# SwiGLU on one core: the first tile loaded with 32 KiB descriptors, all other full tiles with 64 KiB

## The chip, the cores and the metric

The kernel runs on one core of a Trainium2 chip. The time is the device time of one execution in microseconds (us). A kernel's executions are timed in rounds beside executions of the kernel before on the same chip. With one core there is no second die to compare.

## The reference

The input is one float32 matrix of 8192 x 8192 (268.44 MB), the output one of 8192 x 4096 (134.22 MB).

```python
a, b = np.split(x, 2, axis=-1)
silu_b = b / (1 + np.exp(-b))
return a * silu_b
```

## The kernel before

Two rows of the input share one partition, so a tile is 128 partitions x 16,384 floats, or 64 KiB per partition and 8 MiB in all. There are 32 tiles and three buffers. Loads are issued from the sync engine (SP), stores of tiles 0 to 29 from GpSimd, and the last stores again from SP. ScalarE computes SiLU in place, VectorE multiplies in place, and the store reads from the same buffer. A buffer is loaded again when its store has landed.

```python
    def load(i, rows=None):
        if i not in tiles:
            tiles[i] = pool.tile([P, R * M], x.dtype, name="xt")
        lo, hi = (0, R) if rows is None else rows
        nc.sync.dma_start(
            out=tiles[i][:, lo * M : hi * M], in_=xv[i * P : (i + 1) * P, lo * M : hi * M]
        )
    # ... swiglu(i, k): activation (SiLU), then tensor_mul; store(i): dma_start
    for i in range(BUFS):
        load(i)
    for i in range(last):
        for k in range(R):
            swiglu(i, k)
        if i == last - 1:
            swiglu(last, 0)
        store(i)
        nxt = i + BUFS
        if nxt < last:
            load(nxt)
        elif nxt == last:
            load(last, (0, 1))
            load(last, (1, 2))
    # ... the last tile is computed and stored in pieces
```

## Time and profile before

| | before |
|---|---|
| median of the three first runs | 936.34 us |
| span of the profiled run | 934.3 us |
| VectorE, ScalarE, GpSimd busy | 30%, 25%, 2% |
| bytes moved, mean rate over the span | 402.68 MB, 431 GB/s |
| SP's data queue (q1), GpSimd's data queue (q0) | 68.6% and 31.2% of 16 engines' span |

"Share of 16 engines' span" is the time that a queue's packets took, divided by sixteen times the span. Two shares that add up to nearly 100% say that the transfer engines are full, and then it matters little who waits for whom. A packet in the trace is here one descriptor, that is one contiguous run in one partition, and I use the two words for the same thing.

### The profile page before, as it was taken

The page shows a single profiled execution, that of the slowest core. Times are in us where ns is not written, and L with a number is a line of the kernel's source. Part 1 is how long each engine was busy: PE and PEld are TensorE (multiplying, and loading weights), DVE is VectorE, ACT ScalarE, POOL GpSimd, SP SyncE. Part 2 cuts the span into 40 slices and gives each one's busy share as a digit, 9 for nine tenths or more (in the row PEclk, how much of TensorE's full clock was granted, in tenths as well). Part 3 has the DMA queues.
Part 4 walks back from the last instruction along what each step waited for, and adds up shares of the span by engine and source line. Part 5 has one row for each costly group of instructions (what it writes and reads, how often), then busy time and mean ns, then how long its engine had stood idle before and what let it go on. Part 6 is the DMA issues. An engine that isn't in the chain of part 4 may idle for free.

```text
span 934.3 us, 400 instructions
## 1 busy us (share of the span) xinstructions
DVE 283.3 (30%) x65; ACT 229.4 (25%) x66; POOL 16.3 (2%) x34
## 2 busy tenths in 40 slices
DVE  0333312333113332133321333213333133331252
ACT  0323330233311333113331133311333203332041
POOL 0000000000000000000000000000000000000000
DMA  9999999999999999999999999999999999999998
GB/s 404 404 449 426 425 448 424 436 429 446 428 422 441 432 446 424 446 415 453 428 421 456 415 452 421 427 450 415 442 428 441 429 435 428 438 450 414 437 432 383
DMA packets 9507, 402.68 MB, mean 431 GB/s; under 512 B 1056, under 2 KB 1056, under 8 KB 1056
## 3 DMA queue, kind: packets, MB, share of 16 engines
q1 hardware_dynamic: 5184, 276.83, 68.6%
q0 software_dynamic: 4320, 125.83, 31.2%
q14 instruction: 3, 0.02, 0.0%
HBM read 268.44 MB, written 134.22 MB: 431 GB/s over the span
## 4 chain that ended last, share of the span: by engine, by line
DMA 84%; DVE 10%; ACT 4%; issue 1%; DVEq 0%; SPq 0%; ACTq 0%
DMA out_dram<-xt 43%; DMA xt<-in_x_dram 40%; DVE xt L51 10%; ACT xt L50 4%; DVEq L106 0%; SPq L43 0%; ACTq L50 0%; DVEq L51 0%
## 5 line engine op out<-in xcount | busy, mean ns | idle before, releaser
L51 DVE TENSOR_TENSOR xt<-xt 128x4096 f32<-128x4096 f32 (+1 forms) x65 | 283.3, 4359 | 636.9 <-ACT xt L50 633.7
L50 ACT ACTIVATE xt<-xt 128x4096 f32<-128x4096 f32 (+1 forms) x65 | 228.1, 3556 | 687.3 <-DMA xt<-in_x_dram 687.3
L58 POOL DMA_DIRECT2D out_dram<-xt x30 | 16.1, 537 | 854.8 <-DVE xt L51 854.8
L50 ACT ACT_TABLE_LOAD x1 | 1.3, 1283 | 0.7 <-PEq L95 0.7
L95 POOL MEMSET const-float32-0.0<- 128x1 f32 x1 | 0.1, 99 | 0.2 <-issue 0.2
L95 POOL MEMSET const-bfloat16-1.0<- 128x1 bf16 x1 | 0.1, 102 | 0.0
L95 POOL MEMSET const-float32-1.0<- 128x1 f32 x1 | 0.1, 99 | 0.0
L95 POOL MEMSET const-uint8-127<- 128x1 uint8 x1 | 0.1, 99 | 0.0
## 6 DMA issues: line engine op xcount, KB each, us to landing
out_dram<-xt POOLq DMA_DIRECT2D x30, 4096.0 KB, 40.5
xt<-in_x_dram SPq DMA_DIRECT2D x2, 4096.0 KB, 26.4
out_dram<-xt SPq DMA_DIRECT2D x1, 4096.0 KB, 23.8
out_dram<-xt SPq DMA_DIRECT2D x2, 2048.0 KB, 14.5
xt<-in_x_dram SPq DMA_DIRECT2D x31, 33.5
```

What stands on the lines that cost most here:

```text
L50: nc.scalar.activation(out=b, in_=b, func=_SILU)
L51: nc.vector.tensor_mul(out=xt[:, k * half + c0 : k * half + c0 + cw], in0=xt[:, k * M + c0 : k * M + c0 + cw], in1=b,)
L58: (nc.gpsimd if i < last - 1 else nc.sync).dma_start(out=ov[i * P : (i + 1) * P, c0 : c0 + cw], in_=tiles[i][:, c0 : c0 + cw])
L95: nc = _bacc.Bacc("TRN2", target_bir_lowering=False, num_devices=1)
```

## The change

The intent can be read from the diff: only the first tile is cut into smaller descriptors, at the one place where the pipeline has nothing else to do. The loads of the other tiles keep their 64 KiB per partition in one piece.

```diff
         lo, hi = (0, R) if rows is None else rows
+        desc = 4 * M if i == 0 else 4 * R * M
         nc.sync.dma_start(
-            out=tiles[i][:, lo * M : hi * M], in_=xv[i * P : (i + 1) * P, lo * M : hi * M]
+            out=tiles[i][:, lo * M : hi * M],
+            in_=xv[i * P : (i + 1) * P, lo * M : hi * M],
+            max_dma_last_dim=desc,
         )
```

## The prediction

> **What bounds the kernel now.** I began with the header of the page and its parts 1 to 3, to see whether an engine or the transfers set the time.
>
> ```profile
> span 934.3 us, 400 instructions
> DVE 283.3 (30%) x65; ACT 229.4 (25%) x66; POOL 16.3 (2%) x34
> DMA  9999999999999999999999999999999999999998
> DMA packets 9507, 402.68 MB, mean 431 GB/s; under 512 B 1056, under 2 KB 1056, under 8 KB 1056
> q1 hardware_dynamic: 5184, 276.83, 68.6%
> q0 software_dynamic: 4320, 125.83, 31.2%
> ```
>
> The busiest compute engine works 30% of the span, while the 16 DMA engines are at 90% or more in every slice but the last. The two data queues together fill 68.6% + 31.2% = 99.8% of the engines' time. The kernel must read 268.44 MB and write 134.22 MB whatever it does, so the bytes bound it, not a wait. The packet records give the rate of one engine: a 64 KiB packet takes 2,418 ns, a 32 KiB packet 1,213 ns (the same for loads and stores), a 16 KiB packet 611 ns. I counted 3,968, 4,224 (3,840 of them GpSimd's stores) and 256 of these. The sum is 9,594.6 + 5,123.7 + 156.4 = 14,874.7 us, or 929.7 us on each of 16 engines. That is within 5 us of the span of 934.3.
>
> Next I read the chain that ended last, at its start, because the change touches only the first tile.
>
> ```profile
> 0.74 0.38 SPq L43
> 1.13 0.06 issue
> 1.18 43.55 DMA xt<-in_x_dram
> 44.75 3.62 ACT xt L50
> 48.40 4.43 DVE xt L51
> 52.93 4.44 DVE xt L51
> 57.66 41.39 DMA out_dram<-xt
> ```
>
> The first 43.55 us of the chain are not the load of tile 0 but that of tile 1, which waits behind tile 0 in the same queue. ScalarE first starts at 22.72 us, when tile 0 has landed, and the chain doesn't pass through that point. The chain's shares by line (43% stores, 40% loads) name waits for data that moves at the full rate; they don't mean that a shorter latency would pay.
>
> Last, the places where engines move less than full rate, since only those can still be won or lost. Columns: window, its length, DVE, ACT and POOL busy with counts, clock, DMA share, GB/s. Packets are counted lumpily in short windows, so I read only the direction.
>
> ```profile
> 2.00:5.00 3.00, 0.00 (x0) 0.02 (x1) 0.00 (x0) 1.00 0.75 306
> 38.00:43.00 5.00, 0.00 (x0) 0.00 (x0) 0.00 (x0) 1.00 0.98 308
> 100.00:900.00 800.00, 247.81 (x56) 199.43 (x56) 14.39 (x27) 1.00 1.00 434
> ```
>
> Steady state is 434 GB/s for 800 us. There are two dips. At the start, first packets begin between 1.75 and 2.62 us and take 3.06 us in the mean instead of 2.42: 0.64 us of extra latency per engine. Around 38.6 to 43 us, one load packet on each engine takes 3.77 us in the mean instead of 2.42, just before the very first store packet (42.16 us): 1.36 us per engine, once. It is the last packet of tile 1. Later stores show no such dip, presumably because their queue no longer runs empty. Elsewhere I assigned packets to engines by end and start, and found two gaps above 150 ns in the whole run, neither above 310 ns. So all that is left beyond pure movement is about 1.8 us before the first byte, 0.64, 1.36, and some 1.5 us after the last byte (932.8 to 934.3).
>
> **What the Trainium skill says.** "DMA: Bandwidth & Descriptors", section "Where 436 GB/s comes from", gives a fabric ceiling of 435 GB/s for the 16 ports. The 434 above agrees, so this kernel has no rate left to find. The same page, section "Why a DMA increments its semaphore by 16 and not by 1", says that one descriptor moves one contiguous run of the last dimension, and that the number of engines follows from the slowest dimension. The changed load has the form 128x2x8192 in place of 128x16384, so 128 still leads and all 16 engines should be used; it becomes 256 descriptors, 16 per engine instead of 8. The trace of before agrees in so far as 31 full loads left 31 x 128 = 3,968 packets of 64 KiB. Third, section "Queues, rings and completion order" says that each engine alternates between queues by packet, so packet size can set the shares of two queues. No run yet shows that for tile 0, and it has no rival queue: its last completion is at 20.6 us after the first packet, about 22.4 us into the span, and the first store packet comes at 42.16. Fourth, "Perfetto Trace Analysis", section "DMA Instruction — HWDGE (DVE, Sync)", says that the issue seen in the profile is the generation of descriptors. In this trace one issue of 128 descriptors takes 0.33 us (0.38 for the first).
>
> **The change part by part.** The listing of instructions shows the same count and order on every engine; the only difference is the shape of the first load. All other loads have 64 KiB per partition in one piece before and after (the last tile's two halves have 32 KiB anyway), so naming the limit changes nothing there.
>
> Removed: 128 packets of 64 KiB, 8 per engine. Added: 256 packets of 32 KiB, 16 per engine. Two small packets cost 2 x 1,213 = 2,426 ns against 2,418, so 8 ns more per pair. The 611 ns of the 16 KiB packet confirms a fixed 8 to 9 ns per packet (2 x 611 - 1,213 = 9). On each engine that is 8 x 8 = 64 ns. The DMA engines are the bound and never idle, so these 0.06 us go straight to the end.
>
> The second term is the generation of descriptors. If the issue scales with their number, the first one grows from 0.38 to about 0.7 us (an estimate, from the issue durations above). The issues of tiles 1 and 2 come later by 0.3 us, hidden behind 19 us of queued work. Whether the first packet waits for all descriptors of the load is not shown; first packets appear at 1.75 us on most engines, but at 2.62 us on the last. If the engines are fed in turn, twice the descriptors could move the late ones by up to 0.4 us, and lateness persists, since every engine has the same bytes to move. I charge 0.1 us, between none and 0.4.
>
> Nothing is subtracted. Compute waits for the semaphore of the whole tile, not for half of a row, so a smaller descriptor makes nothing available earlier. Sum: +0.06 + 0.1 = about +0.2 us, giving 936.34 + 0.2 = 936.5.
>
> **The rivals.** *A faster start.* The intent may be that the pipeline fills sooner when the first packet is half as long. For it: the first packets are the slow ones. Against it: their excess, 0.19 to 1.02 us by engine, looks like a latency before the first byte, and not like a packet that must be read whole before it is written; for that, the excess would have to be close to 2.4 us. If half the excess did scale with size, the gain would be 0.3 us: 936.0. *A different first store.* The 1.36 us dip could depend on how the queue stands when the first store arrives. For it: it is the largest loss in the run. Against it: tile 0's descriptors are gone 20 us before, and tiles 1 and 2 keep theirs. A different phase could make it 0.5 us shorter or longer: 935.8 to 937.0. *Half the bytes in flight at the start.* If 32 KiB reads kept the memory less busy, tile 0 would load below full rate. The last tile's 32 KiB loads ran at 1,213 ns per packet, that is full rate, so I give this little; at a loss of 2% in tile 0's 19.4 us it would be +0.4 us: 936.7.
>
> **Range and chances.** The three runs of before lie within 0.65 us, so noise is about 0.35 us either way. The rivals move the time by -0.5 to +0.7 us. Together an 8 in 10 range of 935.6 to 937.4. A change of 2% is 18.7 us, about the whole transfer of tile 0; with the bytes unchanged at the ceiling rate I see no way to win that, and a loss would need a fault such as fewer engines. Chances: faster 1%, within 2% 98%, slower 1%.
>
> **What would show it.** In the changed profile: 128 packets of 64 KiB gone and 256 of 32 KiB there, so q1 has 5,312 packets for the same 276.83 MB; tile 0's 32 KiB packets at 1,213 ns after the first; ScalarE's first start within 0.3 us of 22.72; the first issue near 0.7 us (or 0.38, if the issue does not scale); the dip before the first store again about 1.4 us; the last packet ending within 1 us of 932.8. I would be wrong if tile 0 used fewer engines or ran below full rate, if its packets took more than 1,300 ns, or if the engines' order after the start changed such that new gaps of over 0.3 us appeared later on.

## The result, and the profile after

The changed kernel took 935.98 us (median of 6 runs, 935.78 to 936.51). The kernel before took 935.93 us (6 runs, 935.80 to 936.64). The ratio is 1.000, with a 95% interval of 0.9987 to 1.0013. A ratio is the mean time of one kernel's runs over that of the other's of the same rounds, so it is not quite the ratio of the medians. A difference of 0.05 us cannot be told from none.

Lines from the page of the changed kernel (header and parts 2 and 3):

```profile
span 934.7 us, 400 instructions
DMA  9999999999999999999999999999999999999998
DMA packets 9635, 402.68 MB, mean 431 GB/s; under 512 B 1056, under 2 KB 1056, under 8 KB 1056
q1 hardware_dynamic: 5312, 276.83, 68.6%
q0 software_dynamic: 4320, 125.83, 31.2%
```

SP's queue has 5,312 packets instead of 5,184, which are the 128 extra ones, for the same 276.83 MB and the same share. The row of transfer engines is as full as before.

The start of the chain that ended last, of the changed kernel (start, duration, what; some short steps left out):

```profile
0.74 0.44 SPq L44
1.18 0.06 issue
1.24 43.29 DMA xt<-in_x_dram
44.55 3.62 ACT xt L53
48.20 4.43 DVE xt L54
52.73 4.44 DVE xt L54
57.46 41.40 DMA out_dram<-xt
```

Step by step this is the chain of before. The first issue takes 0.44 us instead of 0.38. Tile 1 is ready at 44.55 instead of 44.75 us, and tile 0 (not on this chain) at 22.81 instead of 22.72.

The same three stretches as in the prediction, for the changed kernel (window, length, VectorE, ScalarE and GpSimd busy with counts, clock, DMA share, GB/s):

```profile
2.00:5.00 3.00, 0.00 (x0) 0.02 (x1) 0.00 (x0) 1.00 0.73 273
38.00:43.00 5.00, 0.00 (x0) 0.00 (x0) 0.00 (x0) 1.00 0.96 315
100.00:900.00 800.00, 247.55 (x56) 199.43 (x56) 14.34 (x27) 1.00 1.00 434
```

The 800 us in the middle run at 434 GB/s in both kernels. The two dips at the start stand where they stood. The lower 273 beside 306 in the first window says nothing of the change: a second trace of the kernel before gives 218 there. By the packet records, tile 0 landed 0.08 us later than before (22.44 against 22.36 us).

The packet records of the trace, in two pairs (the second pair was taken later, as r_before and r_after; see the experiments):

| | before | before again | after | after again |
|---|---|---|---|---|
| tile 0's packet, steady duration | 2,418 ns | 2,418 ns | 1,213 ns | 1,213 ns |
| first packets, over the steady duration | 0.64 us | 0.78 us | 0.77 us | 0.59 us |
| tile 0 landed (last engine) | 22.36 us | 22.61 us | 22.44 us | 22.31 us |
| dip at the first store, per engine | 1.36 us | 1.17 us | 1.17 us | 1.19 us |
| last data packet ended | 932.76 us | 933.10 us | 933.22 us | 932.70 us |

"First packets, over the steady duration" is the mean over the 16 engines. "Dip" is the excess of each engine's one stretched load packet over 2,418 ns, averaged over the engines.

Two traces of one and the same kernel differ by up to 0.25 us in the rows of the start and by 0.34 and 0.52 us in the last row, which is more than the change can make. Had I had only the first pair, I could have told a story in which a shorter dip pays for slower first packets. The second pair takes it away.

### The profile page after: what moved, and what is told of

It is laid out like the page before. It is cut to its first block, busy times and chain, and to the rows that moved or that the text cites. A ratio compares the mean times of both kernels' runs of the same rounds, so it can differ in the third digit from the quotient of the medians.

```text
span 934.7 us, 400 instructions
## 1 busy us (share of the span) xinstructions
DVE 283.3 (30%) x65; ACT 229.4 (25%) x66; POOL 16.3 (2%) x34
## 3 DMA queue, kind: packets, MB, share of 16 engines
q1 hardware_dynamic: 5312, 276.83, 68.6%
## 4 chain that ended last, share of the span: by engine, by line
DMA 84%; DVE 10%; ACT 4%; issue 1%; DVEq 0%; SPq 0%; ACTq 0%
DMA out_dram<-xt 43%; DMA xt<-in_x_dram 41%; DVE xt L54 10%; ACT xt L53 4%; DVEq L109 0%; SPq L44 0%; ACTq L53 0%; DVEq L54 0%
```

## The experiments

The theory is that the 16 transfer engines are full from the second to the 933rd microsecond, so a change of descriptors costs or wins the fixed time per packet, times the packets per engine, and nothing else. The rivals are that the start of the pipeline has slack or can be shortened, that packet sizes set the shares of the two queues and so the waits, and that the dip at the first store moves with the change. Each kernel below gave correct results.

### All full tiles in 32 KiB pieces (e1_all_32k)

```diff
-        desc = 4 * M if i == 0 else 4 * R * M
+        desc = 4 * M
```

> All full loads in 32 KiB pieces (31 tiles rather than the first alone). Theory (the engines are full, so each extra packet costs its fixed 8 ns, and nothing else counts): 31 x 8 x 8 ns = 2.0 us more than before, 937.9 against 935.9, with no gaps above 150 ns beyond a handful. Rival (packet size sets the shares of the two queues, and that shapes the waits): loads fall from two bytes in three to one in two while a store is queued, stores land sooner than 40 us after issue, and the time moves by something other than 2 us, more than 4 us either way. Rival (size is free): 935.9, unchanged.

It took 937.55 us (6 runs, 937.42 to 941.53) against 935.94 (11 runs); the ratio of the means is 1.0027 (1.0015 to 1.0040), pulled up by two long runs out of six (939.66 and 941.53). By the medians this is 1.6 us more for 31 tiles, by the means 2.6 us, against 2.0 expected. So one tile's share is 0.05 to 0.08 us. The shares of the queues did change, as the rival had it: SP's waits for a buffer, which were 28.5 to 28.6 us nearly throughout before, now alternate between about 21 and 36 us. But the time did not move by the 4 us or more that this rival needed. The profile fell on the run of 939.66 us, and it shows some twenty-five single packets stretched by 0.25 to 0.84 us between 564 and 915 us, so that the engines ended unevenly (their last completions lie 2.4 us apart, against 1.2 before). Eighteen of them lie where GpSimd's queue starts again after 17 us without a packet (at 564.49, 622.71, 680.79, 738.82, 797.10 and 855.64 us). At the eight earlier starts of this kind, from 99.18 to 506.65 us, no packet was stretched by more than 0.01 us. Why the later ones and not the earlier I do not know.

### All loads in 8 KiB pieces (e2_all_8k)

```diff
-        desc = 4 * M if i == 0 else 4 * R * M
+        desc = 8192
```

> All loads, the last halves too, in 8 KiB pieces. Theory: 28,544 more load packets, at 8 to 9 ns each over 16 engines, 14 to 16 us more: 950 to 952 us, ratio 1.015 to 1.017; an 8 KiB packet takes about 310 ns (9 + 2,409/8). Rival (queue shares): stores now take four bytes in five while both queues have work, the stores land in half the time, loads bunch up, and the time is off that sum by more than 5 us.

It took 951.25 us (4 runs, 951.18 to 951.49) against 935.94, ratio 1.0164 (1.0149 to 1.0178). That is 15.3 us more, in the middle of the expected 14 to 16. An 8 KiB packet took 312 ns. The cost per extra packet is 15.3 x 16 / 28,544 = 8.6 ns, the same 8 to 9 ns as from the packet durations of the first trace. Lines from the page of this kernel (parts 2, 3 and 6; the last is stores: count, KB each, median us from issue to landing):

```profile
DMA  9999999999999999999999999999999999999998
DMA packets 38051, 402.68 MB, mean 424 GB/s; under 512 B 1056, under 2 KB 1056, under 8 KB 1056
q1 hardware_dynamic: 33728, 276.83, 69.7%
q0 software_dynamic: 4320, 125.83, 30.7%
out_dram<-xt POOLq DMA_DIRECT2D x30, 4096.0 KB, 16.6
```

The rival of the queue shares was half right: the stores land in 16.6 us, where the kernel before shows

```profile
out_dram<-xt POOLq DMA_DIRECT2D x30, 4096.0 KB, 40.5
```

and yet the time stays on the packet sum, and not 5 us off it.

The reader should see that a slower kernel looks just as full in the busy row: "9" means that packets were in work, not that they were as large as they could be. Only the GB/s and the packet count tell the two apart. (The rounded shares of its two queues add up to 100.4%, since packets of one engine overlap by some nanoseconds in the records.)

### The first tile alone in 1 KiB and in 8 KiB pieces (e3_first_1k, e3b_first_8k)

```diff
-        desc = 4 * M if i == 0 else 4 * R * M
+        desc = 1024 if i == 0 else 4 * R * M      # e3b: 8192
```

> The change exaggerated: the first tile alone in 1 KiB pieces, 64 per partition, 512 per engine instead of 8. Theory: a cost in tile 0 goes straight to the end although the chain that ended last does not pass through tile 0's landing: 504 extra packets x 8 to 9 ns = 4.0 to 4.5 us, so 940 to 940.5 us, ScalarE's first start 4 us later than 22.7. Rival (tile 0's landing has slack, because the chain starts with tile 1's load): no more than 0.5 us, 936.4. Rival (generation of descriptors is what a smaller piece costs): the first issue grew by 0.06 us for 128 more descriptors; at that price 8,064 more cost 3.8 us in the issue, and if the engines wait for it, the first packets come late.

> The first tile alone in 8 KiB pieces, a middle dose, for the trace only. Theory: 56 extra packets per engine x 8 to 9 ns = 0.5 us, too small for a time but readable in the landing of tile 0 (22.9 us instead of 22.4). The first packet's excess over its steady duration, 0.64 us with 64 KiB and 0.77 us with 32 KiB, should again be 0.6 to 0.8 us if it is a latency before the first byte; under the rival (it scales with the piece) it would be under 0.15 us. The first issue: 0.38 us plus 0.42 if 128 descriptors cost 0.06 each time.

With 1 KiB pieces the kernel took 939.63 us (4 runs, 939.34 to 939.73) against 935.94, ratio 1.0038 (1.0026 to 1.0051): 3.7 us more. That is a little under the 940 to 940.5 us expected. So a delay in tile 0 does go to the end, for the most part, although the chain that ended last does not pass through tile 0's landing. The rival of slack in tile 0 allowed 0.5 us and is refuted. The chain of this kernel starts so:

```profile
0.74 0.42 SPq L44
1.16 0.06 issue
1.22 47.07 DMA xt<-in_x_dram
48.31 3.63 ACT xt L53
```

The load of tile 1 is issued at 1.22 us as before, but takes 47.07 us instead of 43.55, because it stands behind tile 0 in the queue of every engine. That is how a transfer off the printed chain reaches the end: through the shared engines. Tile 0 itself landed at 27.10 instead of 22.36 us (22.61 in the second trace of before), 4.5 to 4.7 us later for 504 extra packets, 9 ns each. The end moved a microsecond less than tile 0 did. The missing part is the dip at the first store: in this trace no load packet before the first store was stretched by more than 0.01 us, while in before it was 1.36 or 1.17. All four timed runs agree with the smaller sum. Why there is no dip here I cannot say (see below).

The issue did not behave as I had supposed. The first issue took 0.42 us, no more than with 256 descriptors (0.44). It was the second issue, of 128 descriptors, that took 20.56 us, the longest of the issues in that line (minimum/median/maximum in ns):

```profile
L44 SPq DMA_DIRECT2D xt<-in_x_dram x33: 327/328/20562, 0.7 to 886.1; - x33
```

All the same the engines were fed: first packets began at 1.82 to 2.01 us, and at every half microsecond from 2.9 us on 16 or more packets were in work. So making the descriptors was not what this kernel waited for; the second issue most likely stood waiting for room behind the first load's 8,192 descriptors, which is an inference. e2_all_8k points the same way: there the third issue took 17.91 us, behind only 2,048 descriptors of the first two loads, so one fixed time per descriptor does not give both waits.

With 8 KiB pieces, one look: 935.72 us, tile 0 landed at 22.83 us (expected 22.9), the first issue took 0.44 us and the next 0.56. The excess of the first packets was 0.43 us in the first packet of each engine and 0.58 us with the stretched second ones added. A packet eight times smaller kept most of the excess, so it is mostly a latency before the data flows. A part that scales with the packet would have left 0.08. The rival of a faster start thus had little ground to win on (one look, and an inference from its trace). The dip was 0.65 us here.

### The intent taken further: tile 0 in two transfers, computed and stored by halves (e4_first_in_halves)

The edit is to the kernel before.

```diff
-    for i in range(BUFS):
-        load(i)
+    load(0, (0, 1))
+    load(0, (1, 2))
+    for i in range(1, BUFS):
+        load(i)
...
             swiglu(i, k)
+            if i == 0:
+                store(0, k * half, half)
...
-        store(i)
+        if i:
+            store(i)
```

> The intent taken to its end: tile 0 loaded by two transfers of 32 KiB per partition, each with its own completion, so that compute starts on the first half, and its two halves stored separately as soon as they are done. Theory (engines full, nothing to gain from earlier work): ScalarE starts near 12.5 us instead of 22.7, the first store is issued near 21 instead of 35.6 us, and the time stays 935.9 +- 0.4. Rival (a quicker start shortens the run): 926 to 930 us. For the dip of 1.36 us before the first store: if it belongs to the first use of GpSimd's queue, it moves with the store to near 24 to 27 us; if it belongs to the last packet of tile 1, it stays at 38.6 us.

It took 937.34 us (5 runs, 937.09 to 938.34) against 936.05 (9 runs), ratio 1.0014 (1.0000 to 1.0027). The first lines of compute and store in its timeline (start, duration, engine, line, what, count, idle before):

```profile
13.02 3.62 ACT L50 ACTIVATE xt<-xt 128x4096 f32<-128x4096 f32 x1 [11.00 <-DMA xt<-in_x_dram]
16.67 4.43 DVE L51 TENSOR_TENSOR xt<-xt 128x4096 f32<-128x4096 f32 x1 [16.67 <-ACT xt L50]
21.41 0.67 POOL L58 DMA_DIRECT2D out_dram<-xt  x1 [20.96 <-DVE xt L51]
```

Compute began at 13.02 instead of 22.72 us and the first store was issued at 21.41 instead of 35.63 us. Nothing came of it: ten microseconds gained at the start are worth nothing when the engines are full anyway. The kernel even lost 1.3 us by the medians, 1.0 us above the range of 935.9 +- 0.4 that I had written; the interval of the ratio just touches 1. In the records, its dips are smaller at the first store (0.29 us on the mean of the engines), but there are two new ones: 0.36 us at 42.7 us, and about 1.0 us on the engines' mean in packets of both queues that start at 75 to 80 us. Just before the second of these, at 70.73 us, the load of tile 2 had landed while SP still waited for the second half of tile 0's store (71.34 us), so for a moment SP's queue was empty. In the kernel before, tile 0's store landed at 69.72 us and tile 2's load only at 73.35, so that queue always had work. The halves also add 16 packets per engine, 0.14 us by the rule above (an estimate). In all the engines end 0.6 us later on their mean than in before, and less evenly (1.75 us apart against 1.15); the rest of the 1.3 us is not accounted for.

### The dip at the first store (e5_warm, e6_store0_sp)

Both are edits to the kernel before.

```diff
 # e5_warm: a tiny transfer on GpSimd's queue, ahead of everything
+    wpool = ctx.enter_context(tc.tile_pool(name="warm", bufs=1))
+    warm = wpool.tile([P, 128], x.dtype, name="warm")
+    nc.gpsimd.dma_start(out=warm[:, :], in_=xv[0:P, 0:128])
 # e6_store0_sp: tile 0's store from SP
-        (nc.gpsimd if i < last - 1 else nc.sync).dma_start(
+        (nc.gpsimd if 0 < i < last - 1 else nc.sync).dma_start(
```

> One tiny transfer of 64 KB on GpSimd's queue at the start, into a scratch tile that nobody reads, ahead of the first store. If the dip of 1.36 us is the price of that queue's first use, it is gone at 38.6 us, and the time falls by up to 1.3 us, to 934.6 (some of it may be paid at the start instead). If it is the price of every store that finds its queue empty, the dip stays 1.3 us and the time 935.9.

> Tile 0 stored by the sync engine's queue instead of GpSimd's; the results are the same. If the dip belongs to the first use of GpSimd's queue, it is absent at 38.6 us and appears when tile 1's store is issued, near 58 to 64 us, with the same 1.3 us. If it belongs to the first store of any kind or to tile 1's last packet, it stays at 38.6 us. Time: tile 0's store now waits behind tile 2's load in one queue, so its buffer comes free slightly later (72 instead of 69 us) and load 3 with it; with tile 1's store to fill the engines 0 to 3 us are lost: 936 to 939 us.

e5_warm: 936.06 us against 936.05, ratio 1.0001 (0.9989 to 1.0014); the dip was 1.14 us. So it is not the price of the queue's first use, at least not one that a load of 64 KB pays. e6_store0_sp: 936.87 us (4 runs, 936.74 to 937.55) against 936.05, ratio 1.0009 (0.9995 to 1.0022), within the expected 936 to 939; the dip was gone from 38 us and was 1.16 us in the packets before 61.46 us, when GpSimd's first store began. These windows of e6_store0_sp show the dip's move, and in the third that it does not come back when GpSimd's next store but one starts:

```profile
38.00:43.00 5.00, 0.00 (x0) 1.01 (x1) 0.00 (x0) 1.00 0.97 419
57.00:62.00 5.00, 0.00 (x0) 0.00 (x0) 0.00 (x0) 1.00 0.91 295
127.00:132.00 5.00, 0.00 (x0) 0.00 (x0) 0.00 (x0) 1.00 1.15 498
```

So the dip goes with GpSimd's first store, wherever that falls, and not with tile 1's load or with stores as such. That the queue had stood empty is not enough. In this same kernel GpSimd's queue moved nothing from 103.51 to 129.30 us and then started beside SP's full queue, with no packet stretched by more than 0.01 us. In e1_all_32k the first store's dip was 1.12 us, and the next eight starts after 17 us without a packet show none; the 29 such starts of e2_all_8k show none either. What is special about the first store is open.

### Two repeats, and the first store held back (r_before, r_after, e7_delay_a, e8_delay_b)

The two repeats are the unchanged kernels. The other two are the kernel before with this edit (1,024 columns in e7, 2,560 in e8):

```diff
+    wpool = ctx.enter_context(tc.tile_pool(name="late", bufs=1))
+    late = wpool.tile([P, 2560], x.dtype, name="late")
...
+        if i == 0:
+            nc.gpsimd.tensor_copy(out=late[:, :1024], in_=tiles[0][:, 2 * half - 1024 : 2 * half])
         store(i)
```

> The kernel before once more, unchanged, for a second trace of it. If the two sub-microsecond differences between the first traces (first packets 0.64 us over their steady duration before and 0.77 after; the dip at the first store 1.36 before and 1.17 after) are spread between executions, this trace lies anywhere within 0.2 us of both pairs; if they belong to the change, it repeats 0.64 and 1.36 within 0.05.

> The changed kernel once more, unchanged. Theory: its 0.06 us cost is below the spread, so the ratio is 1.000 with an interval that holds 1; the first tile's packets are 1,213 ns again and the first issue 0.44 to 0.45 us (against 0.38). If the difference in the dip belongs to the change, it is 1.17 again within 0.05; if it is spread, not.

> Before, with the first store held back on GpSimd by a copy of 1,024 columns of tile 0's product into scratch (an estimate: 1 to 2 us, its duration is read from the trace). If the dip is tied to the end of a load transfer (the store comes due in tile 1's last packet), a delay that carries the store into tile 2's packets shrinks the dip to 0.0 to 0.3 us, as in the runs where the first store fell inside a transfer, and the time falls by about 1 us to 935. If it is tied to the phase between the issue and the end of the current packet, it changes with the delay modulo 2.42 us. If it is a fixed price, it stays 1.2 to 1.4 us.

> The same with 2,560 columns (an estimate: 2.5 times the delay of the 1,024). Same readings as for the shorter delay: tied to the transfer's end, the dip is 0.0 to 0.3 us in both; tied to phase, it differs between the two; fixed, 1.2 to 1.4 us in both. Later issue alone costs nothing, since the engines have tile 2's load to work on: no more than 0.3 us.

r_after took 936.01 us (5 runs, 935.89 to 936.11) against 935.86 (9 runs), ratio 1.0002 (0.9989 to 1.0014), so the change again cannot be told from noise. r_before, one look, took 936.40. Their traces are the columns "again" above, and they settle that the differences in the first packets and in the dip are spread between executions: r_before shows 0.78 and 1.17 us, which are the figures of the changed kernel's first trace. (The dip of r_after, 1.19, would by itself have fitted either reading.)

In e7_delay_a the copy took 1.04 us, the first store was issued at 36.27 us, and the dip was 1.33 us, still in tile 1's last packet; time 936.36 us (4 runs, 936.09 to 936.62), ratio 1.0005 (0.9992 to 1.0019). In e8_delay_b the copy took 2.32 us, the store was issued at 37.60 us and its first packets came at 44.42 us, after a packet of tile 2; the dip was 1.04 us there. So it is not tied to the end of a load transfer either, as I had guessed it might be. It is 1.04 to 1.36 us in nine of the thirteen traces but was 0.65, 0.29, about 0.2 (e2_all_8k) and 0.01 us in the others; what sets its size stays open.

e8_delay_b took 937.72 us (4 runs, 937.53 to 938.74), ratio 1.0022 (1.0007 to 1.0038), where I had allowed 0.3 us. Its trace shows again a second dip, in packets that start at 75 to 81 us, of 1.4 us on the engines' mean, after tile 0's store and tile 2's load had both landed at 71.80 us, that is after SP's queue had run empty. With e4_first_in_halves this makes two cases in which a loss of a microsecond follows the restart of SP's queue after it had stood empty beside a working one. Two cases are an observation, and I did not make a kernel that tests this alone. GpSimd's queue, restarted many times in e1_all_32k and e2_all_8k, lost 0.00 to 0.15 us each time, so it is no rule of queues in general.

## Why the prediction was right

The number was 936.5 us with a range of 935.6 to 937.4, and the chance of "within 2%" was put at 98%. The medians were 935.98 and 936.01. This result alone could not have told the sum of +0.2 us from none: its interval is 1.2 us wide to either side. What supports the working is the larger doses.

**The bound.** Right. The engines were full in every kernel, and adding packets cost what the packet sum said: 15.3 us for 28,544 of them, 1.6 us by the medians for 3,968 (2.0 expected). Two readings were a little off. The gaps above 150 ns in the trace of before are three, not two, and in each (457, 603 and 875 us) the records have a packet of the instruction queue of 0.31 us, so the engine was not idle. And the parts listed, 929.7, 1.8, 0.64, 1.36 and 1.5, add up to 935.0 us, 0.7 more than the span; the recorded packets of one engine overlap by some nanoseconds.

**The packets' term, 0.06 us.** Right as far as it can be seen. The 32 KiB packets took 1,213 ns. The one tile of the change is too small to be measured by itself; what the larger doses show for one tile is 0.05 to 0.08 us, from e1_all_32k divided by 31.

**The issue's term, 0.1 us.** The step "the first one grows from 0.38 to about 0.7 us" was mis-sized. It measured 0.44 us in the changed kernel and 0.42 in its repeat, so 0.04 to 0.06 us for 128 more descriptors; and 0.42 us even for 8,192 descriptors. The profiled length of the first issue did not scale with its descriptors. The first packets began at 1.84 to 2.47 us and in the repeat at 1.81 to 2.94, against 1.75 to 2.62 and 1.76 to 2.44 of before, so the late ones vary by more than the 0.1 us charged, whatever the kernel. Nothing of this term is visible at the end.

**The starting point.** The 936.34 us that I added to came from three runs. Six to eleven runs beside the others gave 935.86 to 936.05. That 0.3 to 0.5 us is the larger part of the difference between 936.5 and 936.0, and the range was wide enough for it.

**"Nothing is subtracted".** Right, and it holds further than I argued. In e4_first_in_halves compute started almost ten microseconds earlier and the time did not fall.

**The rivals.** The faster start fell with e3b_first_8k. The different first store was right to be named as the largest loss in the run, but its size varies between executions of one kernel, and no run shows that the change moves it. "Later stores show no such dip, presumably because their queue no longer runs empty" is not borne out: in e6_store0_sp and e2_all_8k that queue did run empty later, for 26 and 17 us, and hardly a packet was stretched at its next start; and e3_first_1k has no dip even at the first store. "Half the bytes in flight at the start" did not happen: tile 0's packets ran at 1,213 ns, as in steady state, and it landed at 22.44 and 22.31 us (22.36 and 22.61 before).

## What to carry to other kernels

When the data queues' shares add up to the whole span of 16 engines, price a change in packets: extra packets per engine times the fixed cost of one, here 8 to 9 ns. Splitting one 8 MiB tile from 64 into 32 KiB descriptors then costs 0.06 us of 936 (an estimate), while splitting all loads into 8 KiB cost 1.6% here, and starting compute ten microseconds earlier won nothing. Before explaining differences of a few tenths of a microsecond between two traces, take a second trace of each kernel.

## What the Trainium skill lacked or had wrong

- "DMA: Bandwidth & Descriptors", section "Why small descriptors are slow (HBM only)", gives a fixed overhead of about 3 cycles per packet without naming the clock, and no cost in ns for an extra packet of some KiB. The runs here show 8 to 9 ns for each extra packet between 8 and 64 KiB, and about 9 ns at 1 KiB. At 32 KiB loads and stores took the same 1,213 ns.
- "Perfetto Trace Analysis", section "DMA Instruction — HWDGE (DVE, Sync)", lets the profiled issue end when all of its descriptors have been made. Here an issue of 8,192 descriptors showed 0.42 us, hardly more than one of 128 (0.38), and the next issue, of 128 descriptors, showed 20.56 us. The page counts a wait for the descriptor generator as part of an issue, and the 20.56 us may be such a wait; then the first issue ended long before its descriptors were made. e2_all_8k speaks more for a wait for room in the queues, but no run settles it.
- No page has the loss at GpSimd's first store beside a working queue: 1.04 to 1.36 us per engine in nine of thirteen traces, but 0.65, 0.29, about 0.2 and 0.01 us in the others. What sets it is open. Later starts of that queue after 17 to 26 us without packets lost 0.00 to 0.15 us.
